# A Mamba-2, gMLP and ConvFFN trunk on one core: the dt chain on GpSimd, group 0's decay tables ahead, the copy of B before the exponentials

## The chip, the cores and the metric

The kernel runs on one core of one Trainium2 chip. The metric is the device time of one execution in microseconds (us); smaller is better. Engines are called TensorE (PE in the profile; PEld are its weight loads), VectorE (DVE), ScalarE (ACT), GpSimd (POOL) and SyncE (SP, which issues most DMAs).

## What is computed

Two layers over x of 512 tokens by 1024 channels, all float32: a Mamba-2 mixer, a ConvFFN, a gated spatial mixer (gMLP) and another ConvFFN, each followed by a LayerNorm of the residual sum. The change touches the Mamba-2 mixer alone:

```python
zxbcdt = x @ w_in
z, xbc, dt = jnp.split(zxbcdt, [SSM_D_INNER, SSM_D_INNER + SSM_CONV_DIM], axis=-1)
xbc = jax.nn.silu(causal_dwconv(xbc, conv_w, conv_b))
xs, Bm, Cm = jnp.split(xbc, ...)            # 8 groups of 4 heads, state 128
dt = jax.nn.softplus(dt + dt_bias)          # (512, 32 heads)
A = -jnp.exp(a_log)
y = ssd_scan(xs, dt, A, Bm, Cm)             # h_t = exp(dt_t A) h_{t-1} + dt_t B_t x_t, y_t = C_t h_t
y = y + d_skip * xs
y = rms_norm_by_group(y * jax.nn.silu(z)) @ w_out
```

The kernel takes chunks of 128 tokens for the scan: within a chunk a product of C and B, masked and multiplied by a table of decays exp(-(S_i - S_j)), and between the chunks three states.

## The kernel before, in words

Every large product runs in float32 split into a rounded high part and a rest: three matmuls of 512 columns per weight block (lines 126 to 128 for in_proj, 214 to 216 for the output projections). A tile of weights (wraw, 512 KB) is loaded by SyncE (line 78), cast to its high part whi by ScalarE (line 80), and VectorE subtracts to get the low part wlo (line 82). Weights are prepared up to six tiles ahead. An in_proj tile is 24 matmuls into one of eight PSUM banks.

The program is written against a framework that puts the instructions of each engine into a fixed order when the program is built. Among those that its plan holds ready, it takes the one that was written first; what is written under tc.high_priority() goes ahead of the rest. It adds the waits between engines. On the chip each engine works its own list in that order and stops at the first instruction whose inputs are missing. SyncE's list is likewise in order: a DMA that has to wait holds up the DMAs behind it.

The parts that the change and the prediction speak of:

- Lines 342 to 363, the dt chain: the 32 rows of dt for four chunks lie on 128 partitions, 128 tokens each (ps_dt). Softplus is worked out as max(v, 0) plus a series for log(1 + e^-|v|), on slices S, t4, s2, q, v, u of xres. A scan (line 357) gives the running sum S, which four DMAs (line 359) write to scr in HBM; t4 (lines 361, 362) and u = -S (line 363) follow.
- dt_cols, lines 365 to 369: TensorE transposes u, v and t4 into ptdt, ScalarE copies them to tcol. It is called in group 1, after the in_proj tile 4 has been asked for.
- ssd(g), from line 374: for each of 8 groups. It loads R (line 377), four rows of scr spread over all partitions, 1 MB. TensorE makes pcb = C B^T (line 384), the transposes pb of B (line 387) and px of x (line 395). ScalarE makes cd (line 397), the table E (16 Relus, line 401, and an Exp, line 404) and EB (line 407), then copies B's transposes to btok (line 409). VectorE multiplies with the mask and with dt (cbm, xw, xdt). TensorE then makes the states pst from btok and xw (line 429), and py and po (lines 443, 450).
- The loop over groups: for each group four in_proj tiles (tiles 4g to 4g+3), each followed by a convolution (line 178 on ScalarE, line 180 three times on VectorE), then a Silu over the group (line 477). advance() runs the parts of earlier groups' ssd in between.

## Time and profile before

| | us |
|---|---|
| median of 3 runs (lowest, highest) | 1440.32 (1438.73, 1442.22) |
| the profiled execution's own time | 1439.39 |
| its span, first to last instruction | 1437.5 |
| TensorE busy | 1423.6 (99%) |
| VectorE busy | 846.1 (59%) |
| ScalarE busy | 611.5 (43%) |
| GpSimd busy | 23.7 (2%) |

The part of the kernel that the change touches lies between 18 and 300 us of the span. Times in the rows below are from the span's start. In a timeline a row gives the start, the duration, the engine (SPq is SyncE's queue), the line of the kernel, the operation, what is written from what, the shapes and a count; in brackets how long the engine was idle before it and what ended that. Instructions in one group are those of one line, engine and operation.

### The profile page before, as it was taken

The page shows a single profiled execution, that of the slowest core. Times are in us where ns is not written, and L with a number is a line of the kernel's source. Part 1 is how long each engine was busy: PE and PEld are TensorE (multiplying, and loading weights), DVE is VectorE, ACT ScalarE, POOL GpSimd, SP SyncE. Part 2 cuts the span into 40 slices and gives each one's busy share as a digit, 9 for nine tenths or more (in the row PEclk, how much of TensorE's full clock was granted, in tenths as well). Part 3 has the DMA queues.
Part 4 walks back from the last instruction along what each step waited for, and adds up shares of the span by engine and source line. Part 5 has one row for each costly group of instructions (what it writes and reads, how often), then busy time and mean ns, then how long its engine had stood idle before and what let it go on. Part 6 is the DMA issues. An engine that isn't in the chain of part 4 may idle for free.

```text
span 1437.5 us, 17317 instructions
## 1 busy us (share of the span) xinstructions
PE 1423.6 (99%) x6911; PEld 1187.8 (83%) x6911; DVE 846.1 (59%) x1147; ACT 611.5 (43%) x893; POOL 23.7 (2%) x30
## 2 busy tenths in 40 slices
PE   8999999999999999999999999999999999999997
PEld 6788888888889888888888888888888888888886
DVE  6878777565378655554336556446378655554336
ACT  5886677343245433333233433223255433333220
POOL 0000000000000000000000000000000000000001
PEclk9999999999999999999999999999999999999999
DMA  6533322333424332323331432223223333333311
GB/s 219 206 106 129 106 100 74 88 115 122 160 73 123 112 99 92 103 90 101 93 98 59 154 125 88 88 88 118 89 81 127 101 103 93 98 103 118 103 44 59
DMA packets 42864, 152.66 MB, mean 106 GB/s; under 512 B 4760, under 2 KB 6040, under 8 KB 41504
## 3 DMA queue, kind: packets, MB, share of 16 engines
q1 hardware_dynamic: 40240, 143.17, 31.0%
q10 hardware_dynamic: 2544, 8.39, 1.7%
q8 instruction: 54, 0.88, 0.2%
q14 instruction: 26, 0.21, 0.0%
HBM read 149.37 MB, written 2.18 MB: 105 GB/s over the span
## 4 chain that ended last, share of the span: by engine, by line
PE 96%; ACT 1%; DVE 1%; DMA 1%; issue 0%; SPq 0%; DVEq 0%; ACTq 0%
PE ip L126 18%; PE ip L127 18%; PE ip L128 18%; PE acc L216 10%; PE acc L214 10%; PE acc L215 10%; PE pv L576 2%; PE pv L578 2%; PE pv L577 2%; PE psp L636 1%; PE py L443 1%; PE pt L279 1%; PE po L450 1%; PE pst L429 1%; PE pcb L384 0%; PE px L395 0%
## 5 line engine op out<-in xcount | busy, mean ns | idle before, releaser
L126 PE MATMUL ip<-xT_hi,whi 128*128 128x512 f32 (+1 forms) x1264 | 484.4, 383 | 0.0
L128 PE MATMUL ip<-xT_hi,wlo 128*128 128x512 f32 (+1 forms) x1264 | 479.8, 380 | 0.0
L127 PE MATMUL ip<-xT_lo,whi 128*128 128x512 f32 (+1 forms) x1264 | 478.7, 379 | 0.0
L82 DVE TENSOR_TENSOR wlo<-wraw,whi 128x1024 fp32r<-128x1024 f32 x242 | 295.7, 1223 | 297.8 <-ACT whi L80 297.3
L80 ACT CAST whi<-wraw 128x1024 fp32r<-128x1024 f32 x242 | 253.8, 1051 | 355.8 <-PE ip L127 289.3
L126 PEld LDWEIGHTS ip<-xT_hi,whi 128*128 128x128 f32 x1264 | 237.9, 188 | 45.3 <-issue 1.2
L128 PEld LDWEIGHTS ip<-xT_hi,wlo 128*128 128x128 f32 x1264 | 237.7, 188 | 44.6
L127 PEld LDWEIGHTS ip<-xT_lo,whi 128*128 128x128 f32 x1264 | 238.0, 188 | 43.3 <-issue 0.2
L214 PE MATMUL acc<-whi,ahi 128*128 128x512 f32 x608 | 237.3, 390 | 0.0
L216 PE MATMUL acc<-whi,alo 128*128 128x512 f32 x608 | 236.6, 389 | 0.0
L215 PE MATMUL acc<-wlo,ahi 128*128 128x512 f32 x608 | 236.5, 389 | 0.0
L214 PEld LDWEIGHTS acc<-whi,ahi 128*128 128x128 f32 x608 | 114.1, 188 | 24.2 <-issue 0.8
L216 PEld LDWEIGHTS acc<-whi,alo 128*128 128x128 f32 x608 | 114.1, 188 | 23.7
L215 PEld LDWEIGHTS acc<-wlo,ahi 128*128 128x128 f32 x608 | 114.1, 188 | 23.6
L193 DVE TENSOR_TENSOR alo<-h,ahi 128x512 fp32r<-128x512 f32 x44 | 30.4, 691 | 103.4 <-ACT ahi L192 103.4
L192 ACT CAST ahi<-h 128x512 fp32r<-128x512 f32 x44 | 27.4, 623 | 141.7 <-PE acc L215 119.5
L180 DVE SCALAR_TENSOR_TENSOR cv<-ip,ppt,cv 128x511 f32<-128x511 f32 (+2 forms) x90 | 66.9, 744 | 2.0 <-ACT cv L178 1.9
L180 DVE SCALAR_TENSOR_TENSOR gt<-ip,ppt,gt 128x511 f32<-128x511 f32 x88 | 65.7, 746 | 1.6 <-ACT gt L178 0.3
L180 DVE SCALAR_TENSOR_TENSOR ut<-ip,ppt,ut 128x511 f32<-128x511 f32 x88 | 65.7, 746 | 1.3
L563 ACT ACTIVATE gt<-gt 128x512 f32<-128x512 f32 x44 | 27.8, 632 | 82.6 <-DVE gt L180 82.5
L284 ACT ACTIVATE xf<-pt,ppt 128x128 f32<-128x128 f32 x96 | 36.6, 466 | 46.0 <-PE pt L279 43.6
L576 PE MATMUL pv<-whi,xT_hi 128*128 128x512 f32 x128 | 50.0, 390 | 0.0
(138 smaller groups left out, 1073.9 us busy)
## 6 DMA issues: line engine op xcount, KB each, us to landing
wraw<-in_wall_dram SPq DMA_DIRECT2D x242, 512.0 KB
xres<-scr SPq DMA_DIRECT2D x8, 1024.0 KB
xr<-in_x_t_dram SPq DMA_DIRECT2D x8, 256.0 KB
xres<-rscr SPq DMA_DIRECT2D x2, 1024.0 KB
xres<-in_x_tok_dram ACTq DMA_DIRECT2D x1, 2048.0 KB
out_dram<-r SPq DMA_DIRECT2D x8, 256.0 KB
wraw_s<-in_wall_dram SPq DMA_DIRECT2D x8, 128.0 KB
lngf<-in_ln_g_dram ACTq DMA_DIRECT2D x2, 512.0 KB
```

The source lines that it names most:

```text
L80: nc.scalar.copy(hi, raw)
L82: nc.vector.tensor_sub(lo, raw, hi.bitcast(F32))
L126: nc.tensor.matmul(o, whi[:, cs], xT_hi[:, k, lo:hi], start=(k == 0), stop=False)
L127: nc.tensor.matmul(o, whi[:, cs], xT_lo[:, k, lo:hi], start=False, stop=False)
L128: nc.tensor.matmul(o, wlo[:, cs], xT_hi[:, k, lo:hi], start=False, stop=(k == NK - 1))
L180: nc.vector.scalar_tensor_tensor(o[:, s:], ps[:, :T - s], col(c + taps - 1 - s), o[:, s:], ALU.mult, ALU.add)
L193: nc.vector.tensor_sub(lo, self.act(k), hi.bitcast(F32))
L214: nc.tensor.matmul(o, a[0][:, ts_], w[0][:, hs], start=(k == 0), stop=False)
L215: nc.tensor.matmul(o, a[0][:, ts_], w[1][:, hs], start=False, stop=False)
L216: nc.tensor.matmul(o, a[1][:, ts_], w[0][:, hs], start=False, stop=(k == nk - 1))
L284: nc.scalar.activation(xf[:, q, :], pt[:, q * P:(q + 1) * P], AF.Identity, scale=col(c), bias=col(c + 8))
L576: nc.tensor.matmul(ps, xT_hi[:, k, ts_], whi, start=(k == 0), stop=False)
```

## The change

The dt chain is written under tc.high_priority(). ScalarE makes |v| from ps_dt by an Abs, and Exp and Identity follow; the sums and products move from VectorE to GpSimd, as two operations each where VectorE had one fused operation; the reciprocal and the scan stay on VectorE. What loads R and makes cd, E and EB becomes a function decay(g). For group 0 it is called right after dt_cols; for the other groups in ssd, behind the copy to btok, which so stands ahead of their tables.

```diff
--- before.py
+++ after.py
@@ -339,28 +339,33 @@
         S, t4, s2, q, v, u = (xres[:, 3, i * P:(i + 1) * P] for i in range(6))
         ea = small[:, 16:17]
         nsl = small[:, 17:18]
-        nc.scalar.activation(v, ps_dt[:, 0:P], AF.Identity, bias=col(C_DT))
-        nc.vector.scalar_tensor_tensor(u, v, -1.0, v, ALU.mult, ALU.min)
-        nc.scalar.activation(u, u, AF.Exp)
-        nc.scalar.activation(ea, col(C_DT + 1), AF.Exp)
-        nc.vector.tensor_scalar_add(q, u, 2.0)
-        nc.vector.reciprocal(q, q)
-        nc.vector.tensor_mul(u, u, q)
-        nc.vector.tensor_mul(s2, u, u)
-        nc.vector.tensor_scalar_mul(q, s2, 1.0 / 13.0)
-        for c in (11, 9, 7, 5, 3):
-            nc.vector.scalar_tensor_tensor(q, q, 1.0 / c, s2, ALU.add, ALU.mult)
-        nc.vector.scalar_tensor_tensor(q, q, 1.0, u, ALU.add, ALU.mult)
-        nc.vector.tensor_scalar_max(v, v, 0.0)
-        nc.vector.scalar_tensor_tensor(v, q, 2.0, v, ALU.mult, ALU.add)
-        nc.vector.tensor_scalar_mul(u, v, ea)
-        nc.vector.tensor_tensor_scan(S, ones, u, 0.0, ALU.mult, ALU.add)
-        for c in range(NT):
-            nc.sync.dma_start(scr[:, c * P:(c + 1) * P], S[32 * c:32 * c + 32, :])
-        nc.vector.tensor_scalar_mul(nsl, S[:, P - 1:P], -1.0)
-        nc.scalar.activation(t4, S, AF.Exp, bias=nsl)
-        nc.vector.tensor_mul(t4, t4, v)
-        nc.vector.tensor_scalar_mul(u, S, -1.0)
+        gs = nc.gpsimd
+        with tc.high_priority():
+            nc.scalar.activation(u, ps_dt[:, 0:P], AF.Abs, bias=col(C_DT))
+            nc.scalar.activation(u, u, AF.Exp, scale=-1.0)
+            nc.scalar.activation(v, ps_dt[:, 0:P], AF.Identity, bias=col(C_DT))
+            nc.scalar.activation(ea, col(C_DT + 1), AF.Exp)
+            gs.tensor_scalar_add(q, u, 2.0)
+            nc.vector.reciprocal(q, q)
+            gs.tensor_scalar_max(v, v, 0.0)
+            gs.tensor_tensor(u, u, q, ALU.mult)
+            gs.tensor_tensor(s2, u, u, ALU.mult)
+            gs.tensor_scalar(q, s2, 1.0 / 13.0, 1.0 / 11.0, ALU.mult, ALU.add)
+            for c in (9, 7, 5, 3):
+                gs.tensor_tensor(q, q, s2, ALU.mult)
+                gs.tensor_scalar_add(q, q, 1.0 / c)
+            gs.tensor_tensor(q, q, s2, ALU.mult)
+            gs.tensor_scalar(q, q, 1.0, 2.0, ALU.add, ALU.mult)
+            gs.tensor_tensor(q, q, u, ALU.mult)
+            gs.tensor_tensor(v, v, q, ALU.add)
+            gs.tensor_scalar_mul(u, v, ea)
+            nc.vector.tensor_tensor_scan(S, ones, u, 0.0, ALU.mult, ALU.add)
+            for c in range(NT):
+                nc.sync.dma_start(scr[:, c * P:(c + 1) * P], S[32 * c:32 * c + 32, :])
+            gs.tensor_scalar_mul(nsl, S[:, P - 1:P], -1.0)
+            nc.scalar.activation(t4, S, AF.Exp, bias=nsl)
+            gs.tensor_scalar_mul(u, S, -1.0)
+            gs.tensor_tensor(t4, t4, v, ALU.mult)
 
         def dt_cols():
             pt = pst("ptdt")
@@ -371,13 +376,29 @@
         st2 = ExitStack()
         gp = pool(st2, "ssmg")
 
-        def ssd(g, cv):
-            Bt, Ct, x0, x1 = (cv[:, i, :] for i in range(4))
+        decays = {}
+
+        def decay(g):
             R = xsl[:, 4 * (g % 2):4 * (g % 2) + 4, :]
             nc.sync.dma_start(R, bass.AP(
                 tensor=scr.tensor, offset=scr.offset + 4 * g * T, ap=[[0, P], [T, 4], [1, T]]))
             EB = gp.tile([P, 2, 384], F32, tag="EB", bufs=1, name=f"EB{g}")
             cd = small[:, 32 + 16 * (g % 2):48 + 16 * (g % 2)].rearrange("p (h c) -> p h c", h=4)
+            nc.scalar.activation(cd, R[:, :, P - 1::P], AF.Exp, scale=-1.0)
+            E = gp.tile([P, NT, 4, P], F32, tag="E", bufs=1, name=f"E{g}")
+            for c in range(NT):
+                for h in range(4):
+                    nc.scalar.activation(
+                        E[:, c, h, :], R[:, h, c * P:(c + 1) * P], AF.Relu,
+                        bias=tcol[:, 0, c, 4 * g + h:4 * g + h + 1])
+            nc.scalar.activation(E, E, AF.Exp, scale=-1.0)
+            for h in range(2):
+                hs = slice(64 * h, 64 * h + 64)
+                nc.scalar.activation(EB[hs], R[hs, h::2, P:], AF.Exp, scale=-1.0)
+            return EB, cd, E
+
+        def ssd(g, cv):
+            Bt, Ct, x0, x1 = (cv[:, i, :] for i in range(4))
             pcb = pst(f"pcb{g}")
             for c in range(NT):
                 cs = slice(c * P, (c + 1) * P)
@@ -394,19 +415,9 @@
                     for k, xx in enumerate((x0, x1)):
                         nc.tensor.transpose(
                             px[:, c2 * 256 + k * P:c2 * 256 + (k + 1) * P], xx[:, c * P:(c + 1) * P], ident)
-            nc.scalar.activation(cd, R[:, :, P - 1::P], AF.Exp, scale=-1.0)
-            E = gp.tile([P, NT, 4, P], F32, tag="E", bufs=1, name=f"E{g}")
-            for c in range(NT):
-                for h in range(4):
-                    nc.scalar.activation(
-                        E[:, c, h, :], R[:, h, c * P:(c + 1) * P], AF.Relu,
-                        bias=tcol[:, 0, c, 4 * g + h:4 * g + h + 1])
-            nc.scalar.activation(E, E, AF.Exp, scale=-1.0)
-            for h in range(2):
-                hs = slice(64 * h, 64 * h + 64)
-                nc.scalar.activation(EB[hs], R[hs, h::2, P:], AF.Exp, scale=-1.0)
             btok = gp.tile([P, 3, P], F32, tag="btok", bufs=1, name=f"btok{g}")
             nc.scalar.copy(btok, pb[:, 0:384].rearrange("p (c n) -> p c n", c=3))
+            EB, cd, E = decays.pop(g) if g in decays else decay(g)
             cbm = gp.tile([P, NT, P], F32, tag="cbm", bufs=2, name=f"cbm{g}")
             nc.vector.tensor_mul(
                 cbm, pcb.rearrange("p (c i) -> p c i", c=NT), mask.unsqueeze(1).broadcast_to([P, NT, P]))
@@ -472,6 +483,7 @@
                 ps = ip.get(4 * g + k)
                 if g == 1 and k == 0:
                     dt_cols()
+                    decays[0] = decay(0)
                 advance(4 * g + k)
                 conv(cv[:, k, :], ps, C_SC + (4 * g + k) * 5, 4)
             nc.scalar.activation(cv, cv, AF.Silu)
```

## Rows read from the trace of the kernel before

**Rows 1.** The page, part 1: busy us, share of the span, instructions.
```profile
PE 1423.6 (99%) x6911; PEld 1187.8 (83%) x6911; DVE 846.1 (59%) x1147; ACT 611.5 (43%) x893; POOL 23.7 (2%) x30
```

**Rows 2.** Waits of TensorE, whole span: us in total, times, longest.
```profile
PE ps_b L126 <- ACT whi_s L111: 4.7, 1, 4.7
PE pst L429 <- ACT btok L409: 0.6, 1, 0.6
PE ptdt L368 <- DVE xres L363: 0.5, 1, 0.5
...
```

**Rows 3.** Timeline of TensorE at the dt transposes.
```profile
38.32 0.39 PE L127 MATMUL ip<-xT_lo,whi 128*128 128x512 f32 x1
38.54 0.39 PE L128 MATMUL ip<-xT_hi,wlo 128*128 128x512 f32 x1
39.43 0.41 PE L368 MATMUL ptdt<-ident,xres 128*128 128x128 f32 x2 [0.50 <-DVE xres L363]
```

**Rows 4.** Timeline of TensorE at group 0's state products.
```profile
58.08 0.39 PE L128 MATMUL ip<-xT_hi,wlo 128*128 128x512 f32 x1
59.04 1.13 PE L429 MATMUL pst<-xw,btok 128*128 128x256 f32 x4 [0.57 <-ACT btok L409]
```

**Rows 5.** Timeline of VectorE during the dt chain.
```profile
23.99 0.94 DVE L347 RECIPROCAL xres<-xres 128x128 f32<-128x128 f32 x1
...
27.27 1.22 DVE L82 TENSOR_TENSOR wlo<-wraw,whi 128x1024 fp32r<-128x1024 f32 x1
28.40 0.28 DVE L352 SCALAR_TENSOR_TENSOR xres<-xres 128x128 f32<-128x128 f32 x1
...
38.03 0.42 DVE L357 TENSOR_TENSOR_SCAN xres<-ones,xres 128x128 f32<-128x128 f32 x1
```

**Rows 6.** Groups of VectorE from 27 to 38.1 us: busy us, mean ns, idle before.
```profile
L82 DVE TENSOR_TENSOR wlo<-wraw,whi 128x1024 fp32r<-128x1024 f32 x6 | 7.3, 1220 | 0.3 <-ACT whi L80 0.3
L352 DVE SCALAR_TENSOR_TENSOR xres<-xres 128x128 f32<-128x128 f32 x5 | 1.4, 284 | 0.0
```

**Rows 7.** Groups of GpSimd by shape, whole span.
```profile
L492 POOL TENSOR_TENSOR small<-small 128x16 f32<-128x16 f32 x2 | 5.8, 2914 | 334.3 <-DVE small L491 334.3
L607 POOL TENSOR_SCALAR_AFFINE_SELECT wsr<-wsr 128x1024 f32<-128x1024 f32 x1 | 1.1, 1098 | 13.5 <-DMA wsr<-in_w_s_t_dram 13.5
L330 POOL TENSOR_SCALAR_AFFINE_SELECT mask<-ones 128x128 f32<-128x128 f32 x1 | 0.3, 292 | 0.0
```

**Rows 8.** Timelines of GpSimd and VectorE: a power alone, one beside wlo.
```profile
406.63 0.55 POOL L203 TENSOR_TENSOR rs<-rs,small 128x1 f32<-128x1 f32 x1 [64.87 <-DVE rs L202]
426.87 1.39 POOL L203 TENSOR_TENSOR rs<-rs,small 128x1 f32<-128x1 f32 x1 [7.92 <-DVE rs L202]
426.64 1.22 DVE L82 TENSOR_TENSOR wlo<-wraw,whi 128x1024 fp32r<-128x1024 f32 x1
```

**Rows 9.** Timeline of ScalarE: the chain's first step, group 0's tables, the copy.
```profile
22.46 0.37 ACT L342 ACTIVATE xres<-ps_dt,ppt 128x128 f32<-128x128 f32 x1 [0.20 <-PE ps_dt L119]
...
50.16 0.23 ACT L397 ACTIVATE small<-xres 128x16 f32<-128x16 f32 x1 [1.49 <-DMA xres<-scr]
...
58.51 0.48 ACT L409 COPY btok<-pb 128x384 f32<-128x384 f32 x1
```

**Rows 10.** Timeline of SyncE's queue: S to HBM, group 0's R back.
```profile
38.47 1.74 SPq L359 DMA_DIRECT2D scr<-xres  x4
...
41.75 0.33 SPq L377 DMA_DIRECT2D xres<-scr  x1
```

**Rows 11.** Groups of ScalarE from 18 to 100 us: a function table's load.
```profile
L397 ACT ACT_TABLE_LOAD x1 | 1.3, 1283 | 0.0
```

**Rows 12.** Timelines: tile 4's first use; tile 7's wlo and first use.
```profile
33.33 0.39 PE L126 MATMUL ip<-xT_hi,whi 128*128 128x512 f32 x1
...
33.36 1.22 DVE L82 TENSOR_TENSOR wlo<-wraw,whi 128x1024 fp32r<-128x1024 f32 x1 [0.28 <-ACT whi L80]
...
52.75 0.48 PE L126 MATMUL ip<-xT_hi,whi 128*128 128x512 f32 x1
```

## The prediction

> **What bounds the kernel now.** I read the busy shares first, then TensorE's (PE's) waits, then the timelines around the two waits that lie in the changed code. TensorE is busy for 1423.6 of 1437.5 us [rows 1], and its waits in the whole span are few: the longest, 4.7 us, is for the first weights, and the two that belong to the code in the diff are 0.5 us for the dt transposes and 0.6 us for the copy of B [rows 2]. So this change is no matter of adding up the work of VectorE (DVE), ScalarE (ACT) or GpSimd (POOL): what it can give is what those two waits cost, and what it can take is a new wait of TensorE.
>
> The profile's idle time is a little short, since the ends of matmuls are modelled. Start to start, one in_proj matmul follows the last by 0.23 us. The last one of tile 4 starts at 38.54, so the dt transposes could start at 38.77, and start at 39.43: 0.66 us lost [rows 3]. The matmul ahead of the state products starts at 58.08, they could start at 58.31 and start at 59.04: 0.73 us lost [rows 4]. Both together are 1.39 us, 0.10% of the span. A difference of about 0.2%, 2.9 us, is what a measurement of this kernel can tell from no change.
>
> **Where the first wait comes from.** The dt chain begins when ScalarE takes ps_dt at 22.46 [rows 9] and ends with the scan, 38.03 + 0.42 = 38.45 [rows 5]: 16 us, though its middle steps take 0.28 us each. The order of VectorE puts a long instruction (a wlo of 1.22 us or a convolution tap of 0.74) between two of its steps; the step at 28.40 has stood behind the wlo of 27.27 [rows 5]. In the 11.1 us from 27 to 38.1 six wlo's take 7.3 us [rows 6].
>
> **The chain on GpSimd, step by step.** No elementwise 128x128 sum or product runs on GpSimd in this trace, so its price is bounded by the selects and powers that do. A one-input select takes 0.29 us for 128 elements and 1.10 for 1024, which is 0.9 ns an element [rows 7]. I take 0.29 for an operation with one tensor input, and 0.29 + 128 x 0.9 ns = 0.41 for two, because their elements are what differs. From above: the power takes 0.55 us for one element [rows 8] and 2.91 for sixteen [rows 7], 0.158 an element and so 0.39 without any; 0.39 + 2 x 128 x 0.9 ns = 0.62. From below: 0.29 for all.
> - Start 22.46. Abs and Exp on ScalarE, 2 x 0.37 (the duration of the step at 22.46 [rows 9]), then GpSimd's first sum 0.29: 23.49.
> - The reciprocal stays on VectorE: 0.94 [rows 5], and it stands behind whatever runs there, 0 to 1.22; I take half: 25.0.
> - Then 16 operations on GpSimd up to the scan's input, 7 with one tensor input and 9 with two: 7 x 0.29 + 9 x 0.41 = 5.7: 30.7.
> - GpSimd is held up beside wlo. The power that ran with VectorE free took 0.55; the one that started at 426.87, inside a wlo (426.64 to 427.86), took 1.39 and ended 0.40 after it [rows 8]. That is 0.84 more for each wlo; at six in 11 us I count four: 3.4, so 34.1.
> - The scan on VectorE, again half of 1.22 of queue and 0.42: S is there at 35.1 instead of 38.45.
> - nsl and u on GpSimd, 2 x 0.29: u at 35.7, 3.1 us before TensorE asks for it at 38.77. t4's Exp and product add 0.37 + 0.41. **The wait for the dt transposes goes: 0.66 us.**
>
> The Trainium skill, SBUF — State Buffer, section Who interferes with whom, says that GpSimd shares its port pair with VectorE, and that a VectorE instruction with two SBUF inputs and a GpSimd instruction that reads SBUF exclude one another for their whole length. By that rule the later of the two always waits, the wlo's behind GpSimd's steps as well; the one pair of rows on it agrees.
>
> Both ends: with 0.29 for every step and no hindrance S is there at 29.5 (22.46 + 0.74 + 0.29 + 0.94 + 16 x 0.29 + 0.42). With 0.62 for every step, all six wlo's at their full 1.22, full queues of 1.22 twice, and two loads of a function table for the Abs at 1.28 [rows 11], it is 47.4 (22.46 + 0.74 + 2.57 + 0.62 + 1.22 + 0.94 + 9.9 + 7.3 + 1.22 + 0.42).
>
> **What moves with it.** VectorE is rid of 17 short steps at 0.28 or less [rows 6], at most 4.8 us, which no wait of TensorE hangs on; worth nothing by itself. SyncE writes scr as soon as S is there, at 38.47, and asks for group 0's table R at 41.75 [rows 10]. ScalarE stands 1.49 us for R and begins with it at 50.16, 11.7 after S [rows 9]. R is 1 MB behind weight loads on one queue, and those keep their order, so I keep the 11.7: 35.1 + 11.7 = 46.8. tcol, which the first Relu needs too, comes of the dt transposes at 38.8, so it is no hindrance.
>
> **Group 0's tables and the copy of B.** From 50.16 to the copy at 58.51 ScalarE works through the tables of group 0, 8.3 us, and the copy, which TensorE waits for, stands last [rows 9]. In group 0 the copy is not moved ahead of them: decay(0) is written earlier still, and the copy stays behind. What helps is that the tables are 3.4 us earlier: 46.8 + 8.3 = 55.1, then the copy, 55.6, before 58.31. **That wait goes too: 0.73 us.** It goes as soon as the tables are 0.8 us earlier. In groups 1 to 7 the copy does come first, and the tables are 0.48 us later for it; TensorE waits for neither there (no row but the one, [rows 2]), so both count nothing; if the products on the tables were just in time, it would cost up to 7 x 0.48 = 3.4 us.
>
> **Waits that the change adds.** The reciprocal and the scan make VectorE wait for GpSimd, and wlo's and taps are queued behind them; t4's Exp and the 20 steps of decay(0) make ScalarE wait, with casts of weights behind them; scr's four writes are on SyncE's queue ahead of weight loads. The cover is what the weights have in hand: tile 4's wlo begins at 27.27, ends at 28.49 and is used at 33.33; tile 7's ends at 34.58 and is used at 52.75 [rows 5, 12]. 4.8 us early and 18 us later is more than a stall of 3 us; if that cover were gone, each us of stall would be one of TensorE.
>
> **The sum.** 0.66 + 0.73 = 1.39 us less. The profiled execution took 1439.39 with its span of 1437.5, so it would be 1438.0 with a span of 1436.1; the median of the runs lies 0.93 above that execution: 1440.32 - 1.39 = 1438.9 us.
>
> **Rivals.**
> - *The chain is later than TensorE's place for it (slower).* The order on TensorE is fixed when the program is built, so if that order counts on a quicker GpSimd, the dt transposes stand where they stood, and TensorE with all that follows waits for u. From S at 38.2 on there is a wait; the loss passes 2.9 us when the transposes start after 39.43 + 2.9 = 42.3, with S at 41.1 to 41.7. At the upper end (u at 47.4 + 1.24 = 48.7) TensorE loses 48.7 - 39.4 = 9.2 us: 1449.5. Midway between my value and that end, S at 41.3, the loss is some 2.7: 1443. For it: hold-up by wlo has been seen [rows 8], and VectorE is full with wlo's in just this stretch [rows 6]. Against: every quarter of the sum must fall on the dear side, and the chain has 3 us in hand. 0.14.
> - *The waits stay or come back elsewhere (no change).* R may be no earlier because weight loads stand ahead of it on its queue; then only 0.66 goes: 1439.7. Or a freed stretch gives TensorE another wait of the same size, say for VectorE's xdt: 1440.3. For it: the order of every engine is made anew, and TensorE's waits are so short that any one step out of place equals them; 0.19.
> - *Faster by more than 0.2%.* It would need 2.9 us of TensorE's time where 1.39 is lost; a few switches between kinds of matmul could add some tenths. Only the scatter of runs gets there: 1437. 0.04.
> - The forecast, 1438.9, has the rest: 0.63.
>
> **How the numbers follow.** Within 0.2% lie the forecast and the second rival, 0.63 + 0.19 = 0.82; slower 0.14, faster 0.04. The range goes from 1437.0 (the forecast less 1.6, the distance of the lowest of the three runs from their median, and a few tenths for the switches) to 1443.2 (no change and 2.9 us more, where the slower case begins).
>
> **What would show it.** Right: TensorE's row of waits has neither the dt transposes nor the copy of B; the scan ends before 38; GpSimd's steps take 0.3 to 0.4 us and some of them, beside a wlo, over 1 us; ScalarE's first step on R starts 11 to 12 us after the scan; the copy of B in group 0 ends before 58. Wrong: a wait of TensorE at the dt transposes of more than 0.7 us; steps of 0.6 us or more on GpSimd; idle VectorE ahead of the scan for several us with wlo's after it, and TensorE waiting for a weight tile; R landing at 50 in spite of an earlier S.

## The result and the profile after

| | before, us | after, us |
|---|---|---|
| median (lowest, highest) | 1440.32 (1438.73, 1442.22) | 1448.60 (1447.29, 1449.97) |
| ratio after / before, 95% interval | | 1.0058 [1.0047, 1.0070] |
| profiled execution's own time | 1439.39 | 1448.60 |
| its span | 1437.5 | 1446.9 |

The change makes the kernel 8.3 us slower. The forecast was 1438.9 and its range ended at 1443.2.

Part 1 of the page after, beside [rows 1]: TensorE's busy time is up by 3.3 us, GpSimd's by 12.7.
```profile
PE 1426.9 (99%) x6911; PEld 1189.2 (82%) x6911; DVE 842.9 (58%) x1130; ACT 611.6 (42%) x894; POOL 36.4 (3%) x51
```
Waits of TensorE after, whole span (us in total, times, longest), beside [rows 2]:
```profile
PE pst L440 <- ACT btok L419: 4.8, 1, 4.8
PE ps_b L126 <- ACT whi_s L111: 4.7, 1, 4.7
PE pst L440 <- ACT hst L443: 1.7, 2, 1.5
PE pst L440 <- DVE xw L429: 1.0, 1, 1.0
PE ptdt L373 <- POOL xres L367: 0.2, 1, 0.2
```
The wait for the dt transposes fell from 0.5 to 0.2 us in this execution. The one for the copy of B, which was to go, rose from 0.6 to 4.8, and two behind it on group 0's states are new.

Where the time is lost can be read from one landmark in two groups, the product pcb = C B^T. TensorE's timeline after (start, duration):
```profile
49.07 0.94 PE L405 MATMUL pcb<-cv 128*128 128x128 f32 x7
...
56.41 0.39 PE L128 MATMUL ip<-xT_hi,wlo 128*128 128x512 f32 x1
61.64 0.70 PE L440 MATMUL pst<-xw,btok 128*128 128x256 f32 x1 [4.84 <-ACT btok L419]
...
68.02 0.63 PE L127 MATMUL ip<-xT_lo,whi 128*128 128x512 f32 x1
68.44 0.63 PE L128 MATMUL ip<-xT_hi,wlo 128*128 128x512 f32 x1
...
71.86 0.47 PE L127 MATMUL ip<-xT_lo,whi 128*128 128x512 f32 x1
...
84.04 0.83 PE L405 MATMUL pcb<-cv 128*128 128x128 f32 x6
```
The same before:
```profile
50.74 0.72 PE L384 MATMUL pcb<-cv 128*128 128x128 f32 x5
...
74.83 0.94 PE L384 MATMUL pcb<-cv 128*128 128x128 f32 x7
```
At group 0's pcb the changed kernel is 1.67 us ahead (50.74 - 49.07), at group 1's it is 9.21 behind (84.04 - 74.83); from there to the end the distance stays between 9.2 and 9.4. So 10.9 us are lost in this one stretch. The lead at group 0 is not the change's doing: 1.57 us of it are there at ps_dt, ahead of the first changed instruction. A third execution has still more of it, that of the kernel of before with only the copy of B moved, which is the same program up to group 0's tables. The products for ps_dt after, before, and there:
```profile
18.86 1.95 PE L119 MATMUL ps_dt<-xr,wdt 128*32 128x128 f32 x64
```
```profile
20.43 1.96 PE L119 MATMUL ps_dt<-xr,wdt 128*32 128x128 f32 x64
```
```profile
17.92 1.95 PE L119 MATMUL ps_dt<-xr,wdt 128*32 128x128 f32 x64
```
At the start of the kernel matmuls follow each other by 0.43 us and later by 0.23; that switch came at 13.3 us in the profiled execution before, at 10.6 in the one after and at 8.8 in the third. Over all the kernels profiled here ps_dt starts between 17.9 and 20.9. Keep this in mind wherever a wait of TensorE is read from one execution: a TensorE that is ahead waits longer at the first input that does not come earlier with it.

7.4 of the 10.9 us are the three waits at group 0's states (4.84 + 1.55 + 1.03). Another part is TensorE's clock: busy time by stretch after (busy us and count of PE, PEld, DVE, ACT, POOL; then PEclk, the granted clock):
```profile
50.00:56.00 6.00, 6.00 (x35) 5.15 (x33) 0.69 (x1) 6.00 (x18) 0.00 (x0) 1.00 0.42 175
56.00:62.00 6.00, 1.16 (x5) 0.70 (x4) 4.00 (x6) 5.95 (x8) 0.00 (x0) 0.98 0.50 173
62.00:67.00 5.00, 2.42 (x5) 0.98 (x5) 5.00 (x8) 3.31 (x6) 0.00 (x0) 0.50 0.68 197
67.00:71.00 4.00, 4.00 (x10) 3.05 (x10) 4.00 (x8) 0.00 (x0) 0.00 (x0) 0.50 0.29 69
```
Behind the stretch in which TensorE worked for 1.16 of 6 us, the granted clock is 0.50, that is 1.2 of 2.4 GHz, and the in_proj matmuls follow each other by 0.43 us (68.02 to 68.44) where 0.23 is usual. Nine of them do so from 68.02 to 71.86, at 0.20 more each 1.8 us; the rest is in the state products themselves and around them. Before, the granted clock was 1.00 through the whole stretch.

**How the wait comes about.** VectorE's timeline after, around the scan:
```profile
27.46 1.22 DVE L82 TENSOR_TENSOR wlo<-wraw,whi 128x1024 fp32r<-128x1024 f32 x1
35.34 0.42 DVE L362 TENSOR_TENSOR_SCAN xres<-ones,xres 128x128 f32<-128x128 f32 x1 [6.65 <-POOL xres L361]
35.68 1.20 DVE L82 TENSOR_TENSOR wlo<-wraw,whi 128x1024 fp32r<-128x1024 f32 x1
```
ScalarE's, from tile 2's convolution to the copy of B, beside [rows 9]:
```profile
26.54 0.77 ACT L178 ACTIVATE cv<-ip,ppt 128x512 f32<-128x512 f32 x1
37.00 0.40 ACT L366 ACTIVATE xres<-xres,small 128x128 f32<-128x128 f32 x1 [9.69 <-POOL small L365]
37.31 1.99 ACT L80 CAST whi<-wraw 128x1024 fp32r<-128x1024 f32 x2
39.19 0.78 ACT L178 ACTIVATE cv<-ip,ppt 128x512 f32<-128x512 f32 x1
...
43.71 1.28 ACT L489 ACT_TABLE_LOAD   x1 [1.31 <-DVE cv L180]
...
49.54 0.23 ACT L387 ACTIVATE small<-xres 128x16 f32<-128x16 f32 x1
...
57.01 0.84 ACT L397 ACTIVATE EB<-xres 64x768 f32<-64x768 f32 x1
57.88 0.78 ACT L178 ACTIVATE cv<-ip,ppt 128x512 f32<-128x512 f32 x1
58.56 1.03 ACT L80 CAST whi<-wraw 128x1024 fp32r<-128x1024 f32 x1
59.49 0.78 ACT L178 ACTIVATE cv<-ip,ppt 128x512 f32<-128x512 f32 x1
60.17 1.04 ACT L80 CAST whi<-wraw 128x1024 fp32r<-128x1024 f32 x1
61.10 0.48 ACT L419 COPY btok<-pb 128x384 f32<-128x384 f32 x1
```
VectorE stands 6.65 us ahead of the scan and ScalarE 9.69 us ahead of t4's Exp, both with work for the weights and convolutions queued behind. SyncE stands too, 6.7 us ahead of scr's writes. Its queue before, up to scr's writes of [rows 10], and after:
```profile
19.15 17.98 SPq L78 DMA_DIRECT2D wraw<-in_wall_dram  x7
```
```profile
19.28 9.76 SPq L78 DMA_DIRECT2D wraw<-in_wall_dram  x4
35.79 1.74 SPq L364 DMA_DIRECT2D scr<-xres  x4
37.62 2.35 SPq L78 DMA_DIRECT2D wraw<-in_wall_dram  x2
```
Before, seven weight loads were issued by 37.1; after, four by 29.0 and then none until 37.6. The tables' first step now starts at 49.54 without a wait for R, only 0.6 us earlier than in [rows 9]: ScalarE has its backlog first, and group 0's Silu (its table load at 43.71, against 42.55 before) waits 1.31 us for taps that are late on VectorE. And two convolutions and two casts, 3.2 us that before lay ahead of the tables, now lie behind them. So the copy of B runs at 61.10 instead of 58.51, 2.6 us later, while TensorE could have started on the states at 56.64 instead of 58.31. Of the wait of 4.84 us, then, 1.67 is the lead given back, 2.60 the later copy, and 0.57 was there before [rows 4]; the two waits behind it and the clock make 2.6 us into 9.2.

### The profile page after: what moved, and what is told of

The parts are those of the page before. It is cut to its first block, busy times and chain, and to the rows that moved or that the text cites. A ratio compares the mean times of both kernels' runs of the same rounds, so it can differ in the third digit from the quotient of the medians.

```text
span 1446.9 us, 17318 instructions
## 1 busy us (share of the span) xinstructions
PE 1426.9 (99%) x6911; PEld 1189.2 (82%) x6911; DVE 842.9 (58%) x1130; ACT 611.6 (42%) x894; POOL 36.4 (3%) x51
## 4 chain that ended last, share of the span: by engine, by line
PE 94%; ACT 3%; DVE 1%; DMA 1%; POOL 1%; issue 0%; SPq 0%; DVEq 0%; ACTq 0%
PE ip L126 18%; PE ip L127 18%; PE ip L128 18%; PE acc L214 10%; PE acc L216 10%; PE acc L215 10%; PE pv L590 2%; PE pv L588 2%; PE pv L589 2%; PE py L454 1%; PE psp L648 1%; PE pt L279 1%; PE pst L440 1%; ACT E L391 1%; PE po L461 1%; DMA xr<-in_x_t_dram 1%
```

## The experiments

All times are medians in us, ratios are to the kernel of before run on the same chip beside them, with their 95% interval. Code and diffs are cut where a line has three dots. A "stand" is the time in which an engine waits for the dt chain with other work queued behind. The quoted expectations name the theories by letters: S, a stand of VectorE or ScalarE costs the time (SV and SA for the one or the other alone); O, the order around the early tables costs it; W, formed on the way, the preparation of weights is a loop (SyncE loads, ScalarE casts, VectorE makes wlo, and that frees the buffer for SyncE's next load), so a stand of any one engine in it stops all of it.

**The parts one by one.** The chain on GpSimd with priority alone, with ssd as it was before:
```diff
-        nc.vector.scalar_tensor_tensor(u, v, -1.0, v, ALU.mult, ALU.min)
...
+        gs = nc.gpsimd
+        with tc.high_priority():
+            nc.scalar.activation(u, ps_dt[:, 0:P], AF.Abs, bias=col(C_DT))
...
```


> The dt chain as changed (GpSimd, with priority); the order in ssd as before: group 0's tables are made in ssd, ahead of the copy of B. Theory S (ScalarE stands 9.7 us for t4's Exp and VectorE 6.7 us for the scan, because the fixed order has them too early): both waits are still there, so most of the 8.3 us remain, 1445 to 1449. Theory O (what costs is the place of group 0's early tables, ahead of two convolutions on ScalarE, with the copy of B behind those): the loss is gone, 1439 to 1441, and TensorE's wait for the copy is under 1 us.

1444.92, ratio 1.0035 [1.0022, 1.0048]. ScalarE stands 10.7 us, VectorE 6.6, and TensorE waits 4.8 for the copy of B and 1.5 for the dt transposes. More than half of the loss comes with the chain alone. The whole change without the early tables:
```diff
-                    decays[0] = decay(0)
```


> The changed kernel without the early call of decay(0): chain on GpSimd, copy of B ahead of the tables in all groups. Theory S: ScalarE and VectorE stand as long as in the changed kernel, 1444 to 1448. Theory O: 1439 to 1441, no wait of TensorE for the copy of B.

1446.67, 1.0046 [1.0032, 1.0059]; the stands are there (10.3 and 6.6), and TensorE waits 4.9 + 1.3 at the states and again 1.5 at the transposes. The early tables aren't needed for the loss; O alone falls. Of before, only the copy of B ahead of the tables:
```diff
+            btok = gp.tile([P, 3, P], F32, tag="btok", bufs=1, name=f"btok{g}")
+            nc.scalar.copy(btok, pb[:, 0:384].rearrange("p (c n) -> p c n", c=3))
             nc.scalar.activation(cd, R[:, :, P - 1::P], AF.Exp, scale=-1.0)
...
-            btok = gp.tile([P, 3, P], F32, tag="btok", bufs=1, name=f"btok{g}")
-            nc.scalar.copy(btok, pb[:, 0:384].rearrange("p (c n) -> p c n", c=3))
```


> The kernel before with the copy of B ahead of the tables and nothing else. Both theories: TensorE's wait of 0.57 us for the copy goes and nothing comes in its place, 1439.6, or 0.05% less than before, which the rounds can hardly tell from none; the timeline must show the state products starting right behind the last matmul of their tile.

1440.64, 1.0003 [0.9994, 1.0012]: no change. TensorE doesn't wait for the copy any more, and waits 3.1 us for the dt transposes:
```profile
39.56 0.66 PE L368 MATMUL ptdt<-ident,xres 128*128 128x128 f32 x2 [3.14 <-DVE xres L363]
```
The edit isn't what lengthened that wait, for the transposes lie 20 us ahead of the copy. This is the execution whose ps_dt starts at 17.92, 2.51 us before that of [rows 3], and the wait is 2.64 longer: u's step starts at 39.19 in the one and at 39.06 in the other, whenever TensorE arrives. And the change with the chain's steps back on VectorE, priority and early tables kept:
```diff
-        gs = nc.gpsimd
+        gs = nc.vector
```


> The changed kernel with every step of the chain that it gives to GpSimd on VectorE instead; order of the source as changed. If GpSimd as such is the cause (theory S in either form): no engine stands for another in the chain, but the chain has 24 steps in VectorE's queue and S comes some us later than before, TensorE waits for the dt transposes: 1440 to 1444. If it is the new order and arithmetic, whatever the engine: 1447 to 1450.

1447.17, 1.0054 [1.0041, 1.0068]. This is another way to lose the same time: the split steps on VectorE make u late, and TensorE waits 6.6 us at the dt transposes, with the clock at 0.66 from 40 to 50 us. This is the mechanism of the prediction's first rival, on another engine.

**Queueing the waiting steps later.** The scan and what follows it are written outside of the priority and tied behind a convolution, so that VectorE and ScalarE first do what is ready:
```diff
...
+                ends = conv(cv[:, k, :], ps, C_SC + (4 * g + k) * 5, 4)
+                if g == 0 and k == 2:
+                    with tc.issue_after(ends[1]):
+                        dt_scan()
+                        dt_t4()
```
(here ends[1] is tile 2's last tap on VectorE; dt_scan is the scan, scr, nsl and u, dt_t4 the Exp and its product.)

> The changed kernel with the scan alone queued on VectorE behind the convolution of tile 2; t4's Exp may go as early as the plan likes. Theory SA: ScalarE stands at the Exp for 3 us or more and the loss follows it, 1442 to 1446. Theory SV: VectorE stands under 2 us, 1440 to 1442.

1441.06, 1.0008 [0.9999, 1.0017]. The stands are 1.6 us (VectorE), 2.0 (ScalarE) and 1.7 (SyncE), and TensorE has no wait at the states; at the dt transposes it waits 3.3 + 0.6, in an execution whose ps_dt starts at 18.12. With dt_t4 tied one step later still, behind tile 4's convolution on ScalarE:
```diff
...
+                if g == 1 and k == 0:
+                    with tc.issue_after(ends[0]):
+                        dt_t4()
```


> The changed kernel with the scan queued on VectorE behind the second tap row's convolution (tile 2) and t4's Exp queued on ScalarE behind the convolution of tile 4; early tables and the copy as changed. Theory S: the two engines stand under 2 us, TensorE's waits for the copy of B and the states go, 1438 to 1441. Theory O: the early tables still stand ahead of the copy and the convolutions, 1446 to 1449. The forecast's own sum (1.39 us of TensorE's waits gone) would be 1438.9.

1441.96, 1.0013 [1.0004, 1.0022]. Both recover most of the loss, and neither is faster than before: with VectorE at work, its wlo's slow GpSimd's chain (in the first of the two, five of its steps up to the scan's input take over 1 us; after the change it was two), S comes at 39.06 instead of 35.76, and scr's writes go out at 39.09, later than before the change (38.47 [rows 10]). A good part of the chain's speed after the change was bought by VectorE's standing idle for it.

Only the Exp tied behind tile 4's convolution, the scan as in the change:
```diff
...
+        with tc.high_priority():
+            dt_scan()
...
+                if g == 1 and k == 0:
+                    with tc.issue_after(ends[0]):
+                        dt_t4()
```

> The changed kernel with t4's Exp alone queued on ScalarE behind the convolution of tile 4; the scan stays where the changed kernel has it, so VectorE stands about 6.6 us. Theory SA (what reaches TensorE is ScalarE's standing, since convolution, Silu, tcol, tables and the copy of B all pass through it): 1440 to 1443, no wait of TensorE for the copy or the states above 1.5 us. Theory SV (VectorE's standing does it): 1446 to 1449.

1446.64, 1.0050 [1.0037, 1.0064]: it tells nothing apart, since t4 came so late that TensorE waited 6.9 us for it at the third dt transpose. Tied behind tile 3's convolution instead:
```diff
-                if g == 1 and k == 0:
+                if g == 0 and k == 3:
```

> The changed kernel with one step queued later: t4's Exp on ScalarE is put behind tile 3's convolution step instead of ahead of it. Order of VectorE, tables, copy of B as in the changed kernel, which took 1448.6. Theory SA (ScalarE's stand of 9.7 us, with the casts and convolutions behind it, is what TensorE pays for): ScalarE stands under 3 us, TensorE's waits for btok and hst of group 0 (4.8 and 1.5) fall under 1 us, and the time is 1440 to 1443. Theory SV (VectorE's stand of 6.7 us ahead of the scan pays): VectorE still stands over 5 us ahead of the scan, the waits of TensorE at the state products stay near 7 us together, and the time is 1446 to 1449. Were ScalarE to stand at the Exp nearly as long from its new place, nothing is told apart.

1446.94, 1.0048 [1.0034, 1.0061]. ScalarE stands 2.4 us only, VectorE and SyncE 6.7; TensorE waits 3.1 + 1.4 at the states and 2.3 at the transposes. SA falls.

**Freeing the engines one at a time.** ScalarE freed altogether, in its place in the order:
```diff
-            nc.scalar.activation(t4, S, AF.Exp, bias=nsl)
+            nc.scalar.activation(t4, ones, AF.Exp, bias=ea)
```


> The changed kernel with t4's Exp reading a tile of ones with the bias ea, in place of the scan's result and its last column: the Exp has nothing to wait for, and keeps its place in ScalarE's order. t4 and the weights of the states made with it are then not the decays; that part of the computation is left out. Everything else, the early tables and the order of all engines, is as in the changed kernel. Theory SA: ScalarE doesn't stand ahead of the Exp, the convolutions of tiles 4 and 5 come over 6 us earlier, TensorE's waits for btok and hst in group 0 fall under 2 us together, and the time is 1440 to 1443. Theories SV (VectorE's stand ahead of the scan) and O (the order itself: tables and casts queued ahead of the copy of B): TensorE waits 5 us or more there, and the time is 1446 to 1449.

1449.67, 1.0066 [1.0050, 1.0081]: no better than the change. Waits from 18 to 75 us of ScalarE, VectorE and SyncE in this run:
```profile
ACT whi L80 <- DMA wraw<-in_wall_dram: 16.6, 7, 6.9
...
DVE xres L362 <- POOL xres L361: 6.6, 1, 6.6
...
SPq L364 <- DVE xres L362: 6.9, 1, 6.9
```
ScalarE doesn't stand for the chain, but for weights that SyncE hasn't loaded. This is what theory W was formed on. VectorE freed and SyncE in part, ScalarE left (rec is the reciprocal, last the last step on GpSimd ahead of the scan):
```diff
...
-            nc.vector.tensor_tensor_scan(S, ones, u, 0.0, ALU.mult, ALU.add)
+            with tc.issue_after(rec):
+                nc.vector.tensor_tensor_scan(S, ones, ones, 0.0, ALU.mult, ALU.add)
...
-            gs.tensor_scalar_mul(nsl, S[:, P - 1:P], -1.0)
+            with tc.issue_after(last):
+                gs.tensor_scalar_mul(nsl, S[:, P - 1:P], -1.0)
```


> The changed kernel with the scan adding up ones instead of dt, so that it waits for nothing of GpSimd's chain; nsl keeps its place at the end of that chain, so t4's Exp still waits there. The decays are then not those of dt: that part of the computation is left out. VectorE doesn't stand ahead of the scan and SyncE doesn't stand ahead of scr's writes; ScalarE still stands 8 us or more ahead of t4's Exp. Theory W (the loop of weight preparation, load, cast, wlo, stops because VectorE stands at the scan and SyncE at scr): TensorE waits under 2 us at the state products, and the time is 1438 to 1442. If ScalarE's stand alone is enough, TensorE waits 4 us or more there and the time is 1445 to 1449.

1445.03, 1.0036 [1.0023, 1.0050]. ScalarE stands 9.0 us. Waits of TensorE at the states:
```profile
PE pst L442 <- DVE cv L180: 2.7, 1, 2.7
PE pst L442 <- DVE xw L431: 2.7, 1, 2.7
```
VectorE idles 5.6 us all the same, up to a wlo at 39.68. The view names the dt transposes, but this wlo's cast, held behind t4's Exp, ends at 39.67: W's other direction. VectorE alone freed, scr written from GpSimd's result v in place of S:
```diff
-                nc.sync.dma_start(scr[:, c * P:(c + 1) * P], S[32 * c:32 * c + 32, :])
+                nc.sync.dma_start(scr[:, c * P:(c + 1) * P], v[32 * c:32 * c + 32, :])
```


> As the run with the scan of ones, but scr's writes take v, the result of GpSimd's last but one step, in place of S: VectorE is free, SyncE stands 5 us or more ahead of scr, ScalarE stands ahead of t4's Exp as before. The decays are again not those of dt. If SyncE's stand by itself holds up the weights (theory W, its one half): 1444 to 1449, weight casts late. If VectorE's stand is what counts: 1438 to 1442. If the tables' place on ScalarE, ahead of the convolutions of tiles 4 and 5, pays by itself: TensorE waits 4 us or more for the copy of B, with the weights on time.

1449.26, 1.0068 [1.0054, 1.0082]; SyncE stands 7.5, ScalarE 9.2, TensorE waits 5.9 + 1.5 + 0.7 at the states. SyncE alone freed, scr's writes on GpSimd's queue:
```diff
-            for c in range(NT):
-                nc.sync.dma_start(scr[:, c * P:(c + 1) * P], S[32 * c:32 * c + 32, :])
...
+            for c in range(NT):
+                gs.dma_start(scr[:, c * P:(c + 1) * P], S[32 * c:32 * c + 32, :])
```


> The changed kernel with scr's four writes issued by GpSimd, behind u, instead of SyncE: SyncE's loads of weights have no step of the chain ahead of them; VectorE stands 6 to 7 us ahead of the scan as before, ScalarE 9 to 10 us ahead of t4's Exp. Theory W with VectorE's stand enough (the wlo's behind the scan keep the buffers from coming free, so the loads are late all the same): 1444 to 1449. If SyncE's stand is what counts: 1438 to 1442. The planned order of ScalarE differs in one place, tile 4's convolution ahead of the tables, so a fast run here would not tell SyncE from that place.

1445.36, 1.0039 [1.0025, 1.0053]; VectorE stands 6.6, ScalarE 9.8, and SyncE still 1.8 for scr, at R's load. TensorE waits 2.2 + 0.9 at the transposes and 1.1 + 0.8 at the states. All three freed, scr from v by GpSimd:
```diff
...
+            with tc.issue_after(rec):
+                nc.vector.tensor_tensor_scan(S, ones, ones, 0.0, ALU.mult, ALU.add)
...
+            nc.scalar.activation(t4, ones, AF.Exp, bias=ea)
...
+                gs.dma_start(scr[:, c * P:(c + 1) * P], v[32 * c:32 * c + 32, :])
```


> The changed kernel with all three stands taken away: the scan adds up ones right behind the reciprocal, t4's Exp reads ones with the bias ea, and scr's writes are issued by GpSimd from v. The decays are not those of dt: that part of the computation is left out. GpSimd's chain, the early tables and the copy of B behind them on ScalarE stay; tile 5's convolution and two casts are still ahead of that copy. VectorE, ScalarE and SyncE each stand under 2 us for the chain. Theory W (the loop of weight preparation passes through all three engines, so any one that stands stops it): with none standing TensorE waits under 2 us at the state products and the time is 1437 to 1442. If the early tables' order on ScalarE costs by itself, it stays at 1445 to 1449 with the weights on time.

1448.37, 1.0054 [1.0036, 1.0073], but a new stand had come in: scr was written late by GpSimd, and R and tables on R were planned early. Waits of this run:
```profile
ACT small L388 <- DMA xres<-scr: 8.9, 1, 8.9
...
DVE wlo L82 <- ACT whi L80: 20.9, 7, 11.9
...
SPq L384 <- DMA scr<-xres: 10.7, 2, 10.2
```
It is a stand of another cause, at about the same price; TensorE waits 3.0 + 1.5 at the transposes and 1.4 + 1.4 at the states. So the run with the scan of ones once more (ScalarE standing, 1445.03), with t4's Exp freed and nothing else:
```diff
-            nc.scalar.activation(t4, S, AF.Exp, bias=nsl)
+            nc.scalar.activation(t4, ones, AF.Exp, bias=ea)
```


> The run with the scan of ones (1445.03), with one thing more: t4's Exp reads ones with the bias ea, so ScalarE too has nothing to wait for. The order of VectorE and SyncE is the same as in that run, that of ScalarE too but for the place of this one Exp; the tables and tile 5's convolution are still ahead of the copy of B. The decays are not those of dt: that part of the computation is left out. Theory W: ScalarE doesn't stand for GpSimd, VectorE no longer stands 5.6 us for late casts, TensorE waits under 2 us at the state products, and the time falls from 1445 to 1437 to 1442. If the order around the tables costs by itself, it stays at 1444 to 1449 though no engine stands over 3 us for the chain.

1439.62, 0.9999 [0.9989, 1.0009]: 5.4 us gained by one instruction's wait, with the other instructions of VectorE, ScalarE and SyncE in the same order in both runs. All waits of TensorE from 18 to 75 us:
```profile
PE ptdt L375 <- POOL xres L369: 3.9, 1, 3.9
```
None is at the states, though tile 5's convolution and the tables are still ahead of the copy of B. The 3.9 us at the transposes are of one execution, the slowest of its ten (1441.96), and one with an early start (ps_dt at 17.98); u is also late in it, at 40.3, for with VectorE at work GpSimd's chain is slower. The runs in one table (stands in us):

| freed | SyncE | ScalarE | VectorE | ratio |
|---|---|---|---|---|
| none (the change) | 6.7 | 9.7 | 6.7 | 1.0058 |
| ScalarE | 6.9 | 0 | 6.6 | 1.0066 |
| VectorE | 7.5 | 9.2 | 0 | 1.0068 |
| SyncE | 1.8 | 9.8 | 6.6 | 1.0039 |
| VectorE, most of SyncE | 3.5 | 9.0 | 0 | 1.0036 |
| the same and ScalarE | 3.5 | 0 | 0 | 0.9999 |
| all by later queueing | 1.7 | 2.0 | 1.6 | 1.0008 |

SyncE's stand looks worth 3 to 4 us (1448.60 against 1445.36, 1449.26 against 1445.03), but that is not shown: ScalarE's order differs in both pairs (in the second, cd and EB lie behind the Silu in the one run and ahead of it in the other). The clean pair is 1445.03 against 1439.62. It shows what ScalarE's stand costs where VectorE doesn't stand and SyncE stands 3.5 us; the runs with ScalarE freed or nearly freed and the other two standing (1.0066, and 1.0048 with the Exp behind tile 3) show that their stands keep the loss. Two things stay open. A kernel with VectorE alone standing wasn't run. And no run has the changed kernel's own order of ScalarE, two convolutions and two casts between the tables and the copy of B, without a stand; in the clean pair it is one of each, so a smaller cost of that order by itself isn't excluded.

**What the waits are worth.** Before, with the dt transposes asked for behind tile 5 and nothing else:
```diff
-                if g == 1 and k == 0:
+                if g == 1 and k == 1:
```


> The kernel of before with the dt transposes asked for behind in_proj tile 5 instead of tile 4, and nothing else. If the gain of the faster kernel of this study (1437.96, ratio 0.9988) comes from the later transposes, this gives 1437 to 1439; if it needs the copy of B first as well, 1439.5 to 1441. TensorE should not wait at the dt transposes; at the copy of B it may wait up to 0.7 us as before.

1439.15, 0.9998 [0.9990, 1.0007]: in the profiled execution TensorE doesn't wait at the transposes, and waits 2.7 us for the copy of B. It started 2.0 us earlier than the one of [rows 4] (ps_dt at 18.46), and as the transposes no longer take that lead, the copy does. The same with the copy of B first:
```diff
+            btok = gp.tile([P, 3, P], F32, tag="btok", bufs=1, name=f"btok{g}")
+            nc.scalar.copy(btok, pb[:, 0:384].rearrange("p (c n) -> p c n", c=3))
             nc.scalar.activation(cd, R[:, :, P - 1::P], AF.Exp, scale=-1.0)
...
-                if g == 1 and k == 0:
+                if g == 1 and k == 1:
```

> The kernel before with the copy of B first and dt_cols called one in_proj tile later (after tile 5 has been asked for). The looks at e2, e6, e8 and e4 show TensorE reaching the dt transposes about 2 us earlier than in the profile of the kernel before, and e4 waiting 3.1 us there with the granted clock at 0.88 behind it. If that wait is what is left to gain, it goes with this place, for the tables need R, which lands later than tcol anyway: 1436 to 1438.5, no wait of TensorE above 0.7 us between 18 and 80. If TensorE's lead is given back at the states or at py instead: 1440 to 1441.

1437.96, 0.9988 [0.9979, 0.9997]: 0.12% faster than before, the only kernel here whose interval lies below 1. In the profiled execution, a late starter (ps_dt at 20.22), TensorE waits for neither the transposes nor the copy, and its granted clock is 1.00 from 20 to 80. And the changed kernel with the later queueing of the scan and the later transposes:
```diff
...
+                    with tc.issue_after(ends[1]):
+                        dt_scan()
+                        dt_t4()
-                if g == 1 and k == 0:
+                if g == 1 and k == 1:
```

> The changed kernel with the whole tail of the dt chain (scan, nsl, t4's Exp) queued behind tile 2's convolution, and the dt transposes put on TensorE behind in_proj tile 5 instead of tile 4. If the chain on GpSimd and the early tables give nothing beyond what the later transposes give, it is as good as the kernel of before with the copy of B first and the later transposes, which took 1437.96: 1437 to 1439. If the rebuilt order has a cost of its own, it stays at 1440 to 1442. TensorE's waits between 18 and 80 us should be under 1 us together, and its granted clock 0.95 or more between 30 and 80 us.

1441.15, 1.0010 [1.0002, 1.0019], that is 1.4 us slower than before and no better than with the later queueing alone (1.0008). TensorE waits 4.3 us for the copy of B, behind a ScalarE that had stood 4.4 ahead of a cast and 2.0 ahead of the Exp.

## Why the prediction was wrong

- **The chain's end was right, its parts were not.** S was there at 35.76 (forecast 35.1), u at 37.48 (35.7). GpSimd's steps after, alone and beside wlo:
```profile
25.65 1.40 POOL L353 TENSOR_SCALAR xres<-xres 128x128 f32<-128x128 f32 x1
27.13 0.46 POOL L355 TENSOR_TENSOR xres<-xres 128x128 f32<-128x128 f32 x1
27.68 1.39 POOL L356 TENSOR_SCALAR xres<-xres 128x128 f32<-128x128 f32 x1
...
29.70 0.53 POOL L356 TENSOR_SCALAR xres<-xres 128x128 f32<-128x128 f32 x1
...
33.19 0.30 POOL L358 TENSOR_SCALAR xres<-xres 128x128 f32<-128x128 f32 x1
```
  Two inputs took 0.46 (0.41 taken), a sum of one input 0.53 (0.29 taken), there is some 0.09 us between steps (nothing taken), and two steps up to the scan's input were held up to 1.4 (four taken). From the end of the reciprocal to the scan's input that makes 10.8 us where 9.1 were forecast. Against it the chain began 0.7 us earlier, and the scan stood behind nothing, because VectorE stood idle. That the end came out is in part luck: where VectorE is kept at work (the later queueing) S comes at 39.06. The wait for the transposes went in the profiled execution, but two other runs with the same chain (alone, and without the early tables) wait 1.5 us there, so that 0.66 gained for good isn't shown.
- **The step that failed is "Waits that the change adds".** It named all three queues, and then put their cost at nothing by counting "a stall of 3 us", for which it gives no working, against what the weights had in hand. The stands were 6.65 us (VectorE), 9.69 (ScalarE) and 6.7 (SyncE), and the time went up by 8.3 us. It could have been bounded from the prediction's own numbers: the chain on GpSimd was put at 25.0 to 34.1, so a scan that VectorE reaches right behind the reciprocal stands up to 9 us.
- **The cover was argued from the wrong user.** TensorE's use of tiles 4 and 7 [rows 12] was not what came last: TensorE waited for no weight tile in this stretch. What ran out was time on the queues that the copy of B and the state products come through, ScalarE's above all. In the time in which it now stands, ScalarE did casts and convolutions before, ahead of the tables; after, these were left for behind the tables, with the copy of B at their end. The Trainium skill, Perfetto Trace Analysis, section Tensor Engine Instruction (MATMUL, LD_WEIGHTS), says in passing that ScalarE, VectorE and GpSimd are strictly first in, first out; the trace agrees: the cast behind the Exp starts at 37.31, 10 us after the end of the convolution ahead of it.
- **The gain at the copy of B did not come.** The step "tables 3.4 us earlier" took R as what releases them. R was no longer the last to come: ScalarE reached the tables at 49.54, forecast 46.8.
- **Of the sign that was to show this mistake, half appeared**: VectorE idle ahead of the scan with wlo's after it. The other half, TensorE waiting for a weight tile, did not; what it waited for was the copy.
- **The first rival's price was of the right size for the wrong reason.** It gave 1443 to 1449.5 by a late u; u was in time.
- **The two waits' worth agrees, but partly by luck.** The kernel of before with both moved gains 1.7 us (0.12%, interval 0.03 to 0.21%), and 1.39 was counted. Yet the 1.39 was read from one execution with a late start. In the run of the copy alone, with the same chain on VectorE, TensorE started 2.5 us earlier and waited 3.1 us at the transposes where [rows 3] lose 0.66. Neither move alone changes the time (1.0003 and 0.9998). That they have to be made together is suggested by this, not shown, since the intervals overlap.

The priority is not what places the waiting steps early: built without it, the program is the same, instruction for instruction. Why the plan has the scan and the Exp so early stays open; that it does, the order of the timelines shows.

## What to carry to other kernels

Before a step is moved to another engine, list every engine whose in-order queue will wait for that step's result, and work out each stand as the new chain's end less the time at which that queue reaches the waiting instruction; then ask what else goes through that queue, down to the next copy that TensorE needs, and not only the nearest user. Where work runs in a loop over several engines (load, cast, subtract, free the buffer), freeing one of them can show little: with one or two freed, ratios stayed at 1.0036 to 1.0068 (1.0058 with none freed), and the loss went only when all stands were short. And a short wait of TensorE read from one profile is no price: an execution that starts 2 us earlier waits 2 us longer at the first input that has a time of its own.

## What the runs showed of the hardware

- A sum or product with one constant on 128x128 float32 took GpSimd 0.53 to 0.55 us, with two constants in one step 0.30 (line 358), a sum or product of two tiles 0.46. That the step which does more is the shorter one was not expected, and is not explained here.
- Beside a wlo the step with two constants took 1.40 us instead of 0.30 (25.65, line 353), the one with one constant 1.39 instead of 0.53 (27.68, line 356). In the run with all three freed and scr written by GpSimd, one wlo took longer beside a step of GpSimd, 1.52 instead of 1.22, so the hold-up goes both ways:
```profile
33.58 0.47 POOL L355 TENSOR_TENSOR xres<-xres 128x128 f32<-128x128 f32 x1
33.60 1.52 DVE L82 TENSOR_TENSOR wlo<-wraw,whi 128x1024 fp32r<-128x1024 f32 x1 [0.22 <-ACT whi L80]
```
  Which of the two is prolonged can't be told from the recorded starts: here GpSimd's is 0.02 us ahead and the wlo is prolonged, at 25.65 GpSimd's is 0.02 us ahead of a wlo at 25.67 and is itself prolonged.
- Behind and between three waits of TensorE, 7.4 us together, the granted clock was 0.50 from 62 to 71 us, which cost 1.8 us more in the in_proj matmuls alone.
- Two executions of programs that are the same up to there reached ps_dt at 17.92 and at 20.43 us, as their matmuls at the start went over from 0.43 to 0.23 us apart at 8.8 and at 13.3 us. From 4 to 14 us the granted clock is shown as 1.00 in both, so the cause stays open.
